# Attention scores in 64-row halves of the TensorE array, the band mask added by VectorE with the maximum, value products in alternating column halves

## The chip, the cores and the metric

The kernel runs on one core of a Trainium2 chip. A core has five engines with queues of their own: TensorE (matrix products, called PE in the profile; its weight loads are PEld), VectorE (DVE), ScalarE (ACT), GpSimd (POOL) and SyncE (SP, which here only starts DMAs). Each engine works through its own queue in the order in which the program was laid out, and waits on semaphores for the others. Products land in PSUM, everything else lies in SBUF. The metric is the time of one execution on the device in microseconds; the lower, the better. Three runs of the kernel before gave 1540.58 us in the median.

## What is computed

Two layers of a hybrid trunk on 128 context tokens (the prompt) and 256 latent tokens (the sample). Each layer is a feed-forward block, a mixing block of attention, convolution and long convolution, and a second feed-forward block. The change touches the attention alone: eight query heads in two groups of four that share one key and one value head, with 64 features each.

```python
# context tokens (block 0): 128 queries x 128 keys, no mask
s = jnp.einsum('bqgrd,bkgd->bgrqk', qblk, k).astype(F32) * scale
p = softmax(concat([s, sink]))[..., :-1]
o = jnp.einsum('bgrqk,bkgd->bqgrd', p, v)
# latent tokens (blocks 1 and 2): 128 queries x (local keys within +-128, and 128 cached keys)
band = jnp.abs(kj[None, :] - BLOCK - qi[:, None]) <= WINDOW
s_loc = jnp.where(valid, s_loc, NEG_INF)        # valid: band and inside the sequence
p = softmax(concat([s_loc, s_ctx, sink]))
o = p[local] @ v + p[context] @ v_cached
```

All inputs are fp32.

## The kernel before

Prompt and sample are handled together: 384 token columns, features on the 128 partitions. All large products are split into a high and a low part of fp32r and need three passes (`mm3`, L252 to L256); their weights come as a stream of 313 chunks of 512 KB, which ScalarE (L240) and VectorE (L241, `lo`) split. The attention products are plain fp32; TensorE takes such a product in two passes, each with its own weight load, so the profile shows two rows for one call.

A Tile scheduler lays out each engine's order from the priorities of the code and its own estimate of durations. Within the mixing block `PROGRAM` (L41) interleaves generators by hand: input projections, the long convolutions (`hyena`, H, and `conformer`, C, with Fourier products at L633 and L679), scores (A), values (V) and the output projection (W).

`attn_k` (L763) makes the keys. `ks` holds the rotated sample keys and the cached keys for blocks 1 and 2, `kp` the prompt keys for block 0. Each has a slot for each key head g, in which the 64 partitions of the other head are zero: GpSimd clears both tiles (L771, L772), then the real halves are filled.

`scores` (L792) runs over three blocks b of 128 queries and four pairs of heads j. The query tile `st["q"][j]` holds head j of group 0 in partitions 0 to 63 and of group 1 in 64 to 127. With the zero-padded keys, a product over all 128 partitions gives the scores of one group.
- Block 0: one product with 256 columns gives both groups (L804); one VectorE maximum (L818).
- Blocks 1 and 2: for each group a product with 384 columns (L809) and one with the identity that adds the 128x128 mask to one third of it (L810). Both go to an `S` buffer in PSUM, of which there are two. VectorE takes the maximum of each (L820).

VectorE then forms the exponent's bias (L821), and ScalarE reads the scores from PSUM, writes the exponential to `P` and sums it up (L825). An `S` buffer comes free when that is read. When the four pairs are done, the sums are inverted, and VectorE and ScalarE multiply the probabilities (L837, L839).

`values` (L842) runs over the blocks b and their key blocks k (1, 3 and 3). For each group g, TensorE transposes four heads' probabilities into an `at` buffer (L858), and ScalarE copies that to `pt` (L861). Then, for each g, one product with 512 columns (L865) writes 64 of the 128 PSUM partitions: the two groups use the left and the right 64 columns of the array (`tile_position=(0, 64 * g)`). After the last k, ScalarE and VectorE split the result for the output projection (L869, L870).

## Time and profile before

| | |
|---|---|
| median of three runs | 1540.58 us (1539.62 to 1542.72) |
| span of the profiled execution | 1540.7 us |
| TensorE busy (products / weight loads) | 1503.2 us / 1427.3 us |
| VectorE, ScalarE, GpSimd busy | 1117.8, 671.4, 29.8 us |
| attention of layer 0 and layer 1 | about 411 to 491 us and 1144 to 1224 us |

The span is counted from the first to the last instruction of the profiled execution. A row of a group names the line of the kernel, the engine, the operation, what is written and what is read, the size, how often it ran, its busy time and the mean duration of one. Rows of the timeline give the start and the duration of an instruction or of some like ones that were merged. TensorE's ends are modelled, and its products are pipelined: the distance of starts tells more than a duration. Busy time counts moments in which two instructions of one engine overlap once.

### The profile page before, as it was taken

The page shows a single profiled execution, that of the slowest core. Times are in us where ns is not written, and L with a number is a line of the kernel's source. Part 1 is how long each engine was busy: PE and PEld are TensorE (multiplying, and loading weights), DVE is VectorE, ACT ScalarE, POOL GpSimd, SP SyncE. Part 2 cuts the span into 40 slices and gives each one's busy share as a digit, 9 for nine tenths or more (in the row PEclk, how much of TensorE's full clock was granted, in tenths as well). Part 3 has the DMA queues.
Part 4 walks back from the last instruction along what each step waited for, and adds up shares of the span by engine and source line. Part 5 has one row for each costly group of instructions (what it writes and reads, how often), then busy time and mean ns, then how long its engine had stood idle before and what let it go on. Part 6 is the DMA issues. An engine that isn't in the chain of part 4 may idle for free.

```text
span 1540.7 us, 22275 instructions
## 1 busy us (share of the span) xinstructions
PE 1503.2 (98%) x8466; PEld 1427.3 (93%) x8466; DVE 1117.8 (73%) x2082; ACT 671.4 (44%) x1160; POOL 29.8 (2%) x75
## 2 busy tenths in 40 slices
PE   6999999999999999999999999999999999999997
PEld 2799999999977999989999998999997799999997
DVE  5799898886984788886657988766599577655332
ACT  5673332335475562333336322333447556333332
POOL 0101000000000000000000000000000000000000
PEclk9999999999999999999999999999999999999998
DMA  7847776665311347676443777654431134454431
GB/s 277 313 134 259 238 239 225 209 212 171 112 58 57 121 151 236 215 231 206 151 151 121 233 225 227 219 178 152 146 120 62 55 110 148 154 164 151 123 123 41
DMA packets 72122, 258.80 MB, mean 168 GB/s; under 512 B 8176, under 2 KB 9712, under 8 KB 72016
## 3 DMA queue, kind: packets, MB, share of 16 engines
q1 hardware_dynamic: 70832, 252.14, 51.2%
q0 software_dynamic: 1184, 5.24, 0.9%
q8 instruction: 66, 1.08, 0.3%
q14 instruction: 40, 0.33, 0.1%
HBM read 250.80 MB, written 6.55 MB: 167 GB/s over the span
## 4 chain that ended last, share of the span: by engine, by line
PE 67%; DMA 14%; DVE 13%; issue 3%; ACT 1%; SPq 0%; DVEq 0%; POOLq 0%; ACTq 0%
DMA raw<-wmod 13%; PE acc L254 12%; PE acc L256 12%; PE acc L255 12%; PE S L254 7%; PE S L256 7%; PE S L255 7%; DVE junk L315 6%; DVE lo L241 4%; PE sp L633 2%; PE S L809 1%; PE sp L679 1%; DVE t L494 1%; PE acc L865 1%; PE sp L926 1%
## 5 line engine op out<-in xcount | busy, mean ns | idle before, releaser
L241 DVE TENSOR_TENSOR lo<-raw,hi 128x1024 fp32r<-128x1024 f32 x313 | 381.9, 1222 | 173.1 <-ACT hi L240 171.1
L240 ACT CAST hi<-raw 128x1024 fp32r<-128x1024 f32 x313 | 327.1, 1047 | 395.2 <-issue 154.2
L315 DVE SCALAR_TENSOR_TENSOR junk<-raw,cb 128x1024 f32<-128x1024 f32 x256 | 312.8, 1222 | 69.9 <-DMA raw<-wmod 67.6
L256 PE MATMUL acc<-h,lo 128*128 128x384 f32 (+1 forms) x960 | 326.6, 340 | 8.3 <-DVE lo L241 8.3
L254 PE MATMUL acc<-h,hi 128*128 128x384 f32 (+1 forms) x960 | 330.6, 345 | 2.2 <-ACT hi L240 2.1
L255 PE MATMUL acc<-h,hi 128*128 128x384 f32 (+1 forms) x960 | 324.8, 339 | 0.0
L256 PE MATMUL S<-h,lo 128*128 128x384 f32 (+1 forms) x768 | 259.6, 338 | 0.1
L254 PE MATMUL S<-h,hi 128*128 128x384 f32 (+1 forms) x768 | 259.6, 338 | 0.0
L255 PE MATMUL S<-h,hi 128*128 128x384 f32 (+1 forms) x768 | 258.9, 337 | 0.0
L256 PEld LDWEIGHTS acc<-h,lo 128*128 128x128 f32 x960 | 181.2, 189 | 14.1 <-DVE lo L241 13.6
L254 PEld LDWEIGHTS acc<-h,hi 128*128 128x128 f32 x960 | 180.5, 188 | 7.2 <-ACT hi L240 3.2
L255 PEld LDWEIGHTS acc<-h,hi 128*128 128x128 f32 x960 | 180.6, 188 | 1.8 <-issue 0.2
L256 PEld LDWEIGHTS S<-h,lo 128*128 128x128 f32 x768 | 144.7, 188 | 1.9 <-DVE lo L241 1.1
L254 PEld LDWEIGHTS S<-h,hi 128*128 128x128 f32 x768 | 144.2, 188 | 0.6 <-issue 0.3
L255 PEld LDWEIGHTS S<-h,hi 128*128 128x128 f32 x768 | 144.3, 188 | 0.0
L384 ACT ACTIVATE h<-x,mod 128x128 fp32r<-128x128 f32 x96 | 41.5, 453 | 83.0 <-DVE x L426 80.2
L494 DVE TENSOR_TENSOR t<-S,t 128x384 f32<-128x384 f32 x72 | 39.9, 554 | 33.6 <-PE S L256 33.6
L272 ACT CAST P<-t 128x384 fp32r<-128x384 f32 x24 | 12.3, 513 | 81.7 <-DVE t L494 81.7
L256 PE MATMUL acc<-P,lo 128*128 128x384 f32 x120 | 40.6, 338 | 0.4 <-DVE lo L241 0.4
L254 PE MATMUL acc<-P,hi 128*128 128x384 f32 x120 | 40.6, 338 | 0.0
L255 PE MATMUL acc<-P,hi 128*128 128x384 f32 x120 | 40.5, 338 | 0.0
L385 DVE SCALAR_TENSOR_TENSOR h<-x,mod,h 128x128 fp32r<-128x128 f32 x96 | 38.4, 415 | 1.2
(348 smaller groups left out, 2268.9 us busy)
## 6 DMA issues: line engine op xcount, KB each, us to landing
raw<-stream SPq DMA_DIRECT2D x313, 512.0 KB, 3.7
raw<-wmod SPq DMA_DIRECT2D x128, 512.0 KB, 4.5
raw<-wms SPq DMA_DIRECT2D x16, 512.0 KB, 6.7
Hd<-sw POOLq DMA_DIRECT2D x6, 768.0 KB, 6.2
H<-Hd SPq DMA_DIRECT2D x6, 768.0 KB, 5.0
x<-x SPq DMA_DIRECT2D x8, 192.0 KB, 6.5
y<-h SPq DMA_DIRECT2D x6, 256.0 KB, 2.6
cb<-crow SPq DMA_DIRECT2D x2, 512.0 KB, 9.0
```

The source lines that it names most:

```text
L240: nc.scalar.copy(out=hi, in_=raw)
L241: nc.vector.tensor_tensor(out=lo, in0=raw, in1=hi.bitcast(F32), op=ALU.subtract)
L254: nc.tensor.matmul(out, lhsT=w[0], rhs=x[0], start=start, stop=False)
L255: nc.tensor.matmul(out, lhsT=w[0], rhs=x[1], start=False, stop=False)
L256: nc.tensor.matmul(out, lhsT=w[1], rhs=x[0], start=False, stop=stop)
L315: nc.vector.scalar_tensor_tensor(out=self.junk, in0=raw, scalar=1.0, in1=self.cb[:, ci, :], op0=ALU.mult, op1=ALU.mult, accum_out=m[:, 2 * ...
L384: nc.scalar.mul(out=hl[:, 0, a:b], in_=self.x[k][:, a:b], mul=sc)
L385: nc.vector.scalar_tensor_tensor(out=hl[:, 1, a:b], in0=self.x[k][:, a:b], scalar=sc, in1=hl[:, 0, a:b].bitcast(F32), op0=ALU.mult, op1=AL ...
L494: nc.vector.tensor_tensor(out=s, in0=up[:, :T], in1=s, op=ALU.mult)
L633: self.nc.tensor.matmul(U[:, ri * 256:ri * 256 + 256], lhsT=self.cst(("fw", t), 128 * ri, 128)[:k], rhs=src[ri], start=True, stop=True)
L679: nc.tensor.matmul(ps[:, t * 128:(t + 1) * 128], lhsT=Y[t][:, k:k + 128], rhs=self.cst(("iv", t), 128 * ri, 128), start=ri == 0, stop=ri == 1)
L809: nc.tensor.matmul(S[g], lhsT=lhs, rhs=kz[:, g, :], start=True, stop=False)
```

## The change

1. `attn_k` keeps one key tile without padding: key head 0 in partitions 0 to 63, key head 1 in 64 to 127. The two clears on GpSimd, two of four rope sums on VectorE, two of four copies and two of four cache loads in both layers fall away.
2. `scores` takes, for each group g, only the partitions 64g to 64g + 63 of queries and keys, in the upper or the lower 64 rows of the array (`tile_position=(64 * g, 0)`). Block 0 has two products with 128 columns in two `S` buffers in place of one with 256.
3. The mask products with the identity go. VectorE adds the mask with the maximum in one instruction (`tensor_tensor_reduce`, shown as ISA, with a second row for the accumulator) and writes the masked scores to `P`. The exponential then reads `P` in SBUF and no longer PSUM, so the `S` buffer comes free with VectorE's read. The constants hold one row of masks with 640 columns, out of which each block takes 384.
4. `values` splits each product into two of 256 columns, in the order half h = 0 of g = 0 and 1, then half h = 1 of g = 0 and 1.
5. The second product of a pair (and the second to fourth of a value group) has a priority that is raised by 400, and the first one waits by an added dependence (`after`) for the last read of the pair before (scores) or for the second `pt` copy (values). Both together place the members of a group next to each other in TensorE's order.

```diff
+PAIR = 400
-    put("mask0", np.where(q[None, :] <= q[:, None], 0.0, -1e30))
-    put("mask1", np.where(q[None, :] >= q[:, None], 0.0, -1e30))
+    z = np.zeros((128, 128))
+    put("mask", np.concatenate([np.where(q[None, :] >= q[:, None], 0.0, -1e30), z, z,
+                                np.where(q[None, :] <= q[:, None], 0.0, -1e30), z], axis=1))
...
+    def after(self, inst, other):
+        if other is not None:
+            self.tc.add_manual_dep(inst.ins, other.ins.name,
+                                   mybir.DependencyInfo(mybir.DependencyClass.Sync, mybir.DependencyReason.DATA),
+                                   reason="pairs of row or column tiles issue together")
...
-        ks = self.S("kv", (128, 2, NS + PAST))
+        ks = self.S("kv", (128, NS + PAST))
         st["kv"] = self.S("kv", (128, 768))
...
+        kp = st["kv"][:, 0:NP]
+        nc.scalar.copy(out=kp, in_=kr[:, 0:NP])
+        nc.gpsimd.dma_start(out=ks[:, NS:NS + PAST], in_=self.d["ck"][l])
+        self.rope(kr[:, NP:T], [(slice(0, 128), ks[:, 0:NS])])
...
-                if b == 0:
-                    t = self.psum("S")[:, :256].rearrange("p (g k) -> p g k", g=2)
-                    nc.tensor.matmul(t, lhsT=lhs, rhs=kz, start=True, stop=True)
-                    S = [t[:, 0, :], t[:, 1, :]]
-                else:
-                    S = [self.psum("S")[:, :nk * 128] for _ in range(2)]
-                    for g in range(2):
-                        nc.tensor.matmul(S[g], lhsT=lhs, rhs=kz[:, g, :], start=True, stop=False)
-                        nc.tensor.matmul(S[g][:, 128 * (2 - b):128 * (3 - b)], lhsT=self.ident,
-                                         rhs=self.cst("mask%d" % (b - 1)), start=False, stop=True)
+                S = [self.psum("S")[:, :nk * 128] for _ in range(2)]
+                for g in range(2):
+                    p = slice(64 * g, 64 * g + 64)
+                    with self.tc.high_priority(offset=PAIR * g):
+                        mm = nc.tensor.matmul(S[g], lhsT=st["q"][j][p, b * 128:(b + 1) * 128], rhs=kz[p], start=True,
+                                              stop=True, tile_position=(64 * g, 0))
+                    if g == 0:
+                        self.after(mm, read)
...
-                if b == 0:
-                    nc.vector.tensor_reduce(out=mx, in_=t, axis=AX.X, op=ALU.max)
-                for g in range(2) if b else ():
-                    nc.vector.tensor_reduce(out=mx[:, g:g + 1], in_=S[g], axis=AX.X, op=ALU.max)
+                for g in range(2):
+                    if b:
+                        read = nc.vector.tensor_tensor_reduce(out=P[:, g, :], in0=S[g],
+                                                              in1=self.cst("mask", 256 * (2 - b), 384), scale=1.0,
+                                                              scalar=-3.0e38, op0=ALU.add, op1=ALU.max,
+                                                              accum_out=mx[:, g:g + 1])
+                        S[g] = P[:, g, :]
+                    else:
+                        nc.vector.tensor_reduce(out=mx[:, g:g + 1], in_=S[g], axis=AX.X, op=ALU.max)
...
-                    nc.scalar.copy(out=pt, in_=tp)
+                    copied = nc.scalar.copy(out=pt, in_=tp)
                     pts.append(pt)
                 vi = 0 if b == 0 else 1 + k
-                for g in range(2):
-                    nc.tensor.matmul(o[64 * g:64 * g + 64, :], lhsT=st["vt"][:, vi, 64 * g:64 * g + 64], rhs=pts[g],
-                                     start=k == 0, stop=k == nk - 1, tile_position=(0, 64 * g))
+                for h in range(2):
+                    c = slice(256 * h, 256 * h + 256)
+                    for g in range(2):
+                        with self.tc.high_priority(offset=PAIR * (h + g > 0)):
+                            mm = nc.tensor.matmul(o[64 * g:64 * g + 64, c], lhsT=st["vt"][:, vi, 64 * g:64 * g + 64],
+                                                  rhs=pts[g][:, c], start=k == 0 and h == 0, stop=k == nk - 1,
+                                                  tile_position=(0, 64 * g), skip_group_check=True)
+                        if h + g == 0:
+                            self.after(mm, copied)
```

Outside the two mixing blocks the order of TensorE is the same. Within them it moves. Three places follow; one row there is one call (two passes on TensorE for the fp32 products), the line numbers are those of the kernel in question, and a number after a tile's name tells its buffers apart. TensorE, layer 0, around the values of block 0 (`acc_4164`) and the second score pair of block 1 (`S_4091`, `S_4092`), before:

```order
L858 MATMUL at_4172<-csts,P_4025 128x128
L353 MATMUL sp_4270<-ones,cv_4072 128x1 x3
L865 MATMUL acc_4164<-pt_4170,kv_3740 64x512
L865 MATMUL acc_4164<-pt_4177,kv_3740 64x512
L254 MATMUL acc_4226<-h_2510,hi_4229 128x386
L809 MATMUL S_4091<-kv_3739,q_3687 128x384
L810 MATMUL S_4091<-csts 128x128
L809 MATMUL S_4092<-kv_3739,q_3687 128x384
L810 MATMUL S_4092<-csts 128x128
L255 MATMUL acc_4226<-h_2510,hi_4229 128x386
```

The same place after, where the values are `acc_4165`, that score pair is `S_4096` and `S_4097`, and `S_4151` and `S_4152` are the next pair:

```order
L867 MATMUL at_4173<-csts,P_4031 128x128
L810 MATMUL S_4096<-kv_3739,q_3687 128x384
L810 MATMUL S_4097<-kv_3739,q_3687 128x384
L877 MATMUL acc_4165<-pt_4171,kv_3740 64x256
L877 MATMUL acc_4165<-pt_4178,kv_3740 64x256
L877 MATMUL acc_4165<-pt_4171,kv_3740 64x256
L877 MATMUL acc_4165<-pt_4178,kv_3740 64x256
L361 MATMUL sp_4269<-ones,cv_4079 128x1 x3
L810 MATMUL S_4151<-kv_3739,q_3919 128x384
L810 MATMUL S_4152<-kv_3739,q_3919 128x384
```

The score pair has moved ahead of the value products, without the mask products (L810 of before), and the four value pieces stand in alternating halves. VectorE, layer 0, the maxima of that second pair, before:

```order
L820 TENSOR_REDUCE st_4084<-S_4091 128x1
L668 TENSOR_TENSOR ut_4010<-ut_4010 128x256
L820 TENSOR_REDUCE st_4084<-S_4092 128x1
L669 TENSOR_TENSOR ut_4010<-sw_4042 128x256
L821 SCALAR_TENSOR_TENSOR st_4084<-st_4084,nsink_77 128x2
```

And after:

```order
L821 ISA P_4100,st_4089<-S_4096,csts 128x384
L821 ISA st_4089 128x1
L673 TENSOR_TENSOR sw_4049<-sp_4059,H_4015 128x512
L675 TENSOR_TENSOR ut_4014<-sp_4059,H_4015 128x512
L821 ISA P_4100,st_4089<-S_4097,csts 128x384
L821 ISA st_4089 128x1
```

Two 512-column products of the long convolution now stand between the pair's two reads. TensorE, layer 0, the second key block of the values of block 1 (`acc_4282` from `pt_4367` and `pt_4374`), before:

```order
L865 MATMUL acc_4282<-pt_4367,kv_3740 64x512
L809 MATMUL S_4404<-kv_3739,q_3921 128x384
L810 MATMUL S_4404<-csts 128x128
L254 MATMUL sp_4378<-cv_4352,hi_4382 128x384
L254 MATMUL sp_4379<-cv_4352,hi_4382 128x384
L809 MATMUL S_4405<-kv_3739,q_3921 128x384
L865 MATMUL acc_4282<-pt_4374,kv_3740 64x512
```

And after, where they are `acc_4281` from `pt_4366` and `pt_4373`:

```order
L867 MATMUL at_4415<-csts,P_4196 128x128
L877 MATMUL acc_4281<-pt_4366,kv_3740 64x256
L877 MATMUL acc_4281<-pt_4373,kv_3740 64x256
L877 MATMUL acc_4281<-pt_4366,kv_3740 64x256
L877 MATMUL acc_4281<-pt_4373,kv_3740 64x256
L867 MATMUL at_4422<-csts,P_4090 128x128
```

The two halves, which stood five products apart, now stand together. Such a separation is found three times in the order before (once in layer 0, twice in layer 1) and not in the order after.

## Rows read from the trace of the kernel before

**Rows 1.** The page's first part: busy us, share of the span, instructions

```profile
PE 1503.2 (98%) x8466; PEld 1427.3 (93%) x8466; DVE 1117.8 (73%) x2082; ACT 671.4 (44%) x1160; POOL 29.8 (2%) x75
```

**Rows 2.** Busy us by stretch: PE, PEld, DVE, ACT, POOL, then PE clock, DMA

```profile
431.00:451.00 20.00, 20.00 (x102) 15.86 (x101) 17.92 (x44) 14.65 (x46) 0.89 (x1) 1.00 0.01 5
451.00:471.00 20.00, 19.35 (x101) 13.12 (x99) 16.00 (x45) 15.15 (x40) 0.00 (x0) 1.00 0.18 54
471.00:491.00 20.00, 19.09 (x94) 12.82 (x94) 7.71 (x20) 11.09 (x27) 0.00 (x0) 1.00 0.17 52
1164.00:1184.00 20.00, 19.58 (x97) 15.10 (x96) 18.37 (x45) 15.07 (x45) 1.24 (x1) 1.00 0.09 27
1184.00:1204.00 20.00, 20.00 (x105) 13.29 (x104) 15.71 (x47) 15.52 (x41) 0.56 (x1) 1.00 0.09 27
```

**Rows 3.** TensorE's waits, 395 to 530 us: total us, times, longest

```profile
PE acc L254 <- DVE h L870: 0.9, 1, 0.9
```

**Rows 4.** TensorE's timeline: one score pair of block 1, one of block 0

```profile
442.13 0.81 PE L809 MATMUL S<-kv,q 128*128 128x384 f32 x2
...
443.00 0.81 PE L809 MATMUL S<-kv,q 128*128 128x384 f32 x2
443.65 0.38 PE L810 MATMUL S<-csts 128*128 128x128 f32 x2
...
1144.61 0.59 PE L804 MATMUL S<-kv,q 128*128 128x256 f32 x2
1145.04 0.38 PE L633 MATMUL sp<-ut,csts 128*128 128x256 f32 x1
```

**Rows 5.** TensorE's timeline: products in four column quarters, at the start

```profile
25.24 0.64 PE L284 MATMUL at<-raw,scond 128*32 128x256 f32 x8
25.81 0.70 PE L926 MATMUL sp<-kv,cv 128*128 128x512 f32 x1
```

**Rows 6.** TensorE's timeline: products that use 8 of the rows

```profile
62.60 0.34 PE L256 MATMUL acc<-h,lo 128*128 128x386 f32 x1
62.77 0.34 PE L256 MATMUL S<-h,lo 128*128 128x386 f32 x1
63.04 0.69 PE L633 MATMUL sp<-P,csts 8*128 8x256 f32 x2
...
64.44 0.59 PE L633 MATMUL sp<-cv,csts 8*128 8x256 f32 x2
64.96 0.44 PE L254 MATMUL acc<-h,hi 128*128 128x386 f32 x1
```

**Rows 7.** Timeline: a joint value group, then one half that stands alone

```profile
1217.44 1.07 ACT L861 COPY pt<-at 128x512 f32<-128x512 f32 x2 [1.80 <-PE at L858]
...
1218.08 1.56 PE L865 MATMUL sp<-pt,kv 128*64 128x512 f32 x4
1218.57 0.19 PEld L865 LDWEIGHTS sp<-pt,kv 128*64 128x64 f32 x2 [0.30 <-ACT pt L861]
1219.57 0.31 PEld L858 LDWEIGHTS at<-csts,P 128*128 128x128 f32 x3 [0.81 <-issue]
...
1195.26 1.07 PE L865 MATMUL acc<-pt,kv 128*64 128x512 f32 x2
1196.26 0.33 PE L858 MATMUL at<-csts,P 128*128 128x128 f32 x1
```

**Rows 8.** VectorE: two groups by line and form, then its timeline

```profile
L820 DVE TENSOR_REDUCE st<-S 128x1 f32<-128x384 f32 x32 | 17.6, 554 | 7.5 <-PE S L810 6.8
L315 DVE DVE_READ_ACCUMULATOR junk<-raw,cb 128x1 f32 x256 | 21.1, 83 | 0.0
...
455.63 1.73 DVE L837 TENSOR_SCALAR P<-P,st 128x384 f32<-128x384 f32 x5
457.28 0.55 DVE L820 TENSOR_REDUCE st<-S 128x1 f32<-128x384 f32 x1
```

16 lines of the change are left out of this document (5 added, 11 removed).

## Prediction

> **What bounds the kernel now.** I read the page first, then the busy time by stretch around the two attention stages, then what TensorE waited for there, and last single instructions. The page says that TensorE is busy for 98% of the span and VectorE for 73% [rows 1]. Busy alone proves little, so the next view matters more: where the attention of layer 0 (431 to 491 us) and of layer 1 (1164 to 1204 us) lies, TensorE is busy for 19.1 to 20 of every 20 us at a granted clock of 1.00, which is the 2.4 GHz level [rows 2]. The waits agree: in layer 0's stage the longest wait of a TensorE product was 0.9 us, once [rows 3]. So TensorE's queue sets the end, and a microsecond of TensorE work that goes away here brings the end forward by as much, as long as no other engine becomes late. The candidate for that is in the same rows: VectorE is busy for 17.92 of 20 us, then 16.00, then only 7.71; in layer 1 18.37 in the first such stretch [rows 2]. The order of TensorE outside the two stages is unchanged, so everything else is taken as it was.
>
> **Scores of blocks 1 and 2 (16 pairs in both layers).** Each fp32 product is two passes. Before, one head pair is two times (a 384-column product over a zero-padded K and a 128-column mask product with the identity). The row starts 442.13 and 443.00 give 0.87 us for one group of heads, 1.73 us for both, and of that the two 384-column passes take 0.65 us (443.00 to 443.65), 0.32 us each [rows 4]. The change drops the mask products and puts the two groups into the upper and lower 64 rows of the array. What remains is two 384-column products in different halves. If the halves run side by side this is 2 x 0.32 = 0.65 us, and no longer 1.73.
>
> Side by side is not shown for row halves, but it is for column quarters and halves: eight 256-column passes in four column quarters took 0.57 us to the next instruction, where one after the other eight of 0.21 us would be 1.7 us [rows 5]. And in the value product the second column half's weight load started at 1218.57, 0.05 us after the end of the copy that it reads (1217.44 plus two copies in 1.07 us would be 1218.51), while the first half was still in its second pass [rows 7]. So a half waits for its data and not for the other half.
>
> Against this stands a price that the old scores didn't pay: a change of the array's partition. It can be read where the kernel multiplies only 8 rows, which also uses a part of the rows. Full-array passes follow each other at 0.17 us (62.60 to 62.77), so the last one ends near 62.94; the next row starts at 63.04, and it lasts 0.10 us longer than the same pair later, which is its weight load. That is 0.20 us of nothing. On the way back the last part-row pass, of which two together take 0.43 us, ends near 64.87, and the next full one streams from 64.96 + 0.10, as it too lasts 0.10 us longer than its like at 62.77: 0.20 us [rows 6]. Together 0.40 us for each visit. In between, passes of 256 columns came 0.215 us apart, so weight loads stay hidden in that mode.
>
> A pair therefore costs 0.65 + 0.40 = 1.05 us instead of 1.73: 0.68 us saved, 16 times, 10.9 us of TensorE work. "TensorEngine Tiling (Array Packing)" of the Trainium skill (Tiling Modes, Key Properties) says the same against this change: switching the tiling mode drains TensorE. The trace agrees and prices it, 0.40 us for a visit.
>
> **Scores of block 0 (8 pairs).** Before, one 256-column product: 0.43 us from 1144.61 to 1145.04 [rows 4]. After, two of 128 columns side by side, 0.22 us, plus 0.40: 0.62. This part loses 0.2 us each, 1.6 us in all: the zero padding was cheaper than the switch.
>
> **Values (14 groups: one and three and three key blocks in two layers).** They already sit in column halves, so the switch is paid now too. A joint group takes 1.49 us from 1218.08 to 1219.57; a half that stood alone took 1.00 us from 1195.26 to 1196.26 [rows 7]. In the new order the four 256-column pieces always stand together and the first waits for the second copy, so both halves start together and need what one half needs, 1.0 us. That is 0.49 us for each of the 11 groups that stood together. In the order, 3 groups had their halves apart (one is shown); each pays two visits of about 1.2 us, and 1.2 us goes. Sum 11 x 0.49 + 3 x 1.2 = 9.0 us. The cover it needs: while the second copy (0.5 us) is under way, TensorE must have something else; at the places that I read in the order a score pair (1.05 us) or four transposes stand there. Without that cover the 0.49 us is not saved, since today's group also ends 1.0 us after the second copy. The split into column halves itself should give nothing, as the halves overlap already.
>
> **VectorE.** 32 maxima of 384 columns (0.55 us each) become 32 add-and-max instructions of the same size with an accumulator read. The nearest row for an operation that also accumulates is the modulation product with its read of 83 ns [rows 8]. Instructions overlap: five that began at 455.63 end 1.73 us later, at 457.36, and the next starts at 457.28, so one occupies about 0.08 us less than its duration [rows 8]. I take 0.47 us as before plus 0.08 us: 0.55. The lower bound is 0.47 (the read is hidden), the upper one twice the columns' time, 0.95 us (a sum and a maximum in two passes, as two separate rows would take). Added to VectorE: 32 x 0.08 = 2.6 us; the eight block-0 maxima become 16 of half the size, which adds about 1 us; four rope sums become two of full height, which takes off half as much. ScalarE's exponentials read the masked copy: no change taken, as ScalarE is at 73 to 78% of these stretches [rows 2]. GpSimd loses four clears, SyncE's constant load grows by 384 columns far ahead of its use: nothing.
>
> **What TensorE's savings run into.** The new order makes the first half of a pair wait until both maxima of the pair before are read, and TensorE's queue is in order: the weights' products, transposes and value products behind it wait too. By the order of VectorE, one or two 512-column spectral products stand between the two reads. So I take the stage in stretches.
>
> The block-0 stretch loses 4 x 0.2 = 0.8 us in each layer. In 431 to 471 us there are 7 pairs (4.8 us) and two joint and one split group (2.2 us): TensorE's work falls from 40 to 33.0 us. VectorE has 17.92 + 16.00 = 33.9 us there [rows 2], with 14 x 0.08 more 35.0. So VectorE becomes the limit, and the stretch can't be shorter than 35.0. It has been 90% busy in a stretch in which TensorE waited for nothing, and I take 95% for one in which TensorE does wait: 35.0 / 0.95 = 36.9, a gain of 3.1 of the 7.0 us. The bounds are 0 and 5.0. From 471 to 491 VectorE is at 39%, and one pair and four groups give their full 0.68 + 4 x 0.49 = 2.6 us. Layer 0: -0.8 + 3.1 + 2.6 = 4.9 us. Layer 1 has VectorE at 18.37 and 15.71 [rows 2], 34.1 us, and the same pieces in slightly other places (two split groups, one group fewer behind): 3.1 again, 2.2 behind, 4.5 us. Sum 9.4 us.
>
> The profiled execution has a span of 1540.7 us and the median is 1540.6, so the sum needs no correction: **1531 us**.
>
> **Rivals.**
> - *A half starts only after the other's last pass has started.* Then a pair is three passes, 0.97 + 0.40 = 1.37 us, and block 0 pays 0.1 us more each. "TensorE: Matmul & The Clock Gate" (Part 3) states such an order: matmuls start and end strictly in program order. The row of 1218.57 doesn't decide it, as that half waited for its copy. In the long stretch TensorE would need 7 x 0.32 = 2.3 us more, 35.3, about what VectorE needs, so some 0.5 us more a layer; with 0.3 us behind and 0.4 us of block 0 that is 2.4 us in both layers: 1533.5.
> - *Row halves don't overlap.* Four passes and a switch, 1.69 us, save 0.04 us a pair, and block 0 costs 0.83 instead of 0.43. Long stretch 0.3 + 2.2 = 2.5, behind 2.0, block 0 -1.6: 2.9 us a layer, 1535. The column rows [rows 5] speak against it.
> - *The waits for the pair's reads eat the whole of the long stretch.* Left are -0.8 + 2.4 us a layer: 1537.4. For it speaks that VectorE is already at 80 to 92% there; against it that the score bank is now free after the maximum and no longer after the exponential, which comes later.
> - *Slower: the add-and-max is a long instruction.* Every pair waits for two of them, so VectorE's 33.9 us grow by 14 times the extra. At 0.95 us instead of 0.47 that is 40.6 us, at 95% 42.8: 2.8 us lost, with block 0 and the end of the stage +1.2 us a layer, 1543. At 1.35 us it is 46.2, or 48.7: +7 us a layer, 1555. It decides from about 0.85 us an instruction. Nothing in the trace has such a length for 384 columns (0.55 us is usual), but this instruction is not in the trace.
>
> **How the numbers follow.** A measurement of this kernel tells 0.2% (3.1 us) from no change. Forecast (1526 to 1534): 0.46; the ordered start 0.10; no overlap 0.10; waits eat it 0.17; slower 0.14; VectorE packs without a gap (5.0 instead of 3.1 us and shorter waits for copies, 1525 or below) 0.03. Of the eaten case, 0.04 lies below 1537.5 and 0.13 around no change; of the slower one 0.01 lies within 0.2%. Faster 0.46 + 0.10 + 0.10 + 0.03 + 0.04 = 0.73, same 0.14, slower 0.13. The range 1525 to 1541 leaves out 0.03 below and 0.13 above.
>
> **What the profile after would show.** Right: the two halves' starts of a pair some 10 ns apart, the pair over 1.1 us after the last full pass; value groups 1.0 us each; VectorE at 95% in the long stretch and TensorE's waits there naming the new add-and-max line, 3 to 5 us a layer; the rest of the kernel shifted without change. Wrong: starts of the second half 0.32 us (ordered) or 0.65 us (no overlap) later; the add-and-max near 1 us; or waits of 7 us and more in a layer.

## The result and the profile after

The changed kernel takes 1519.5 us (median of 4 executions, 1515.2 to 1519.9) beside 1540.1 us for the kernel before on the same chip: a ratio of 0.985, 95% interval 0.984 to 0.987. That is 20.6 us less where the forecast had 9.6 less; the range 1525 to 1541 missed it on the fast side. The profiled execution took 1519.2 us with a span of 1517.4 us, 23.3 us under the span before.

The first page line after answers [rows 1]: TensorE is busy for 16.8 us less, VectorE as long as before.

```profile
PE 1486.4 (98%) x8474; PEld 1416.0 (93%) x8474; DVE 1116.1 (74%) x2120; ACT 671.6 (44%) x1158; POOL 26.8 (2%) x69
```

The busy time by stretch answers [rows 2] (columns as there: PE, PEld, DVE, ACT, POOL, then PE clock, DMA share, GB/s). The stages come earlier now, layer 1's by about 20 us.

```profile
431.00:451.00 20.00, 19.08 (x101) 12.38 (x99) 19.99 (x67) 16.84 (x48) 1.93 (x1) 1.00 0.09 27
451.00:471.00 20.00, 19.09 (x119) 14.49 (x118) 17.81 (x57) 17.98 (x49) 0.00 (x0) 1.00 0.09 27
471.00:491.00 20.00, 19.84 (x127) 17.10 (x125) 8.67 (x20) 10.14 (x20) 0.00 (x0) 1.00 0.32 99
1144.00:1164.00 20.00, 18.80 (x92) 12.63 (x92) 17.84 (x52) 13.90 (x41) 0.00 (x0) 0.91 0.08 27
1164.00:1184.00 20.00, 17.40 (x103) 10.62 (x102) 16.21 (x55) 16.97 (x46) 0.89 (x1) 1.00 0.09 27
1184.00:1204.00 20.00, 19.57 (x121) 15.73 (x120) 9.74 (x26) 11.51 (x27) 0.00 (x0) 1.00 0.25 80
```

VectorE fills 37.8 of the 40 us from 431 to 471 us (95%), and TensorE, which was busy for 39.4 of them before, now stands idle for 1.8. In layer 1 the idle share is larger, and the granted clock of 1144 to 1164 us is 0.91 where it was 1.00 throughout.

Single instructions on TensorE (start, duration, operation) answer [rows 4] and [rows 7]: a score pair of block 1, a pair of block 0, and a value group.

```profile
433.21 0.34 PE L262 MATMUL acc<-h,hi 128*128 128x386 f32 x1
433.39 0.34 PE L263 MATMUL acc<-h,hi 128*128 128x386 f32 x1
433.67 0.92 PE L810 MATMUL S<-kv,q 64*128 64x384 f32 x4
434.51 0.44 PE L264 MATMUL acc<-h,lo 128*128 128x386 f32 x1
434.79 0.34 PE L262 MATMUL acc<-h,hi 128*128 128x386 f32 x1
...
408.37 0.34 PE L264 MATMUL acc<-h,lo 128*128 128x386 f32 x1
408.64 0.49 PE L810 MATMUL S<-kv,q 64*128 64x128 f32 x4
409.06 1.13 PE L641 MATMUL sp<-ut,csts 128*128 128x256 f32 x4
...
473.04 1.08 PE L877 MATMUL sp<-pt,kv 128*64 128x256 f32 x8
474.05 0.66 PE L867 MATMUL at<-csts,P 128*128 128x128 f32 x4
```

Full passes follow each other at 0.18 us (433.21 to 433.39), so the next was due at 433.57. The pair starts 0.10 us later, takes 0.84 us, and the pass behind it lasts 0.10 us longer than its like (434.51 to 434.79): 1.04 us from one regular pass to the next. In the unmerged records the two halves' first passes start 6 to 7 ns apart, then both second ones 0.43 us later. A block-0 pair takes 0.42 us and 0.10 on entry. A value group takes 1.01 us.

VectorE (first the instructions of the add-and-max line with least, median and longest ns, then its timeline) answers [rows 8]:

```profile
L821 DVE CUSTOM_DVE_ANT_0 P<-S,csts x32: 544/550/558, 435.5 to 1186.1; 128x384 f32<-128x384 f32 x32
L821 DVE DVE_READ_ACCUMULATOR2_ANT st<- x32: 77/83/85, 435.9 to 1186.6; 128x1 f32 x32
...
445.30 0.56 DVE L821 CUSTOM_DVE_ANT_0 P<-S,csts 128x384 f32<-128x384 f32 x1
445.78 0.08 DVE L821 DVE_READ_ACCUMULATOR2_ANT st<- 128x1 f32 x1
445.78 0.55 DVE L821 CUSTOM_DVE_ANT_0 P<-S,csts 128x384 f32<-128x384 f32 x1
```

The add-and-max is as long as the old maximum (550 against 554 ns), and the read of its accumulator runs beside the next instruction: 0.48 us from start to start.

**Where the time went.** I compare when the same weight product starts in both traces (7512 of them, in the same order). The difference, after minus before, at the edges of the stretches:

| stretch (us of before) | what runs there | shift at its end, us | gained there, us |
|---|---|---|---|
| 0 to 396 | start, first feed-forward | -3.1 | 3.1 |
| 396 to 503 | mixing with attention, layer 0 | -11.0 | 7.9 |
| 503 to 906 | feed-forward (the gain lies in 636 to 720) | -13.5 | 2.6 |
| 906 to 991 | feed-forward, layer 1 | -20.8 | 7.3 |
| 991 to 1097 | feed-forward | -20.8 | 0.0 |
| 1097 to 1235 | mixing with attention, layer 1 | -23.3 | 2.5 |
| 1235 to the end | feed-forward | -23.3 | 0.0 |

The two mixing blocks give 10.4 us. The other 12.9 us come from stretches in which not one instruction was changed or moved, but for the longer load of the constants in the first. The 3.1 us of the first stretch say nothing, though: in a second profiled execution of the changed kernel (a_same, below) that stretch was 3.0 us longer than before. The granted clock stood at the 1.2 GHz level (0.50) for 10.2 us of it, against 3.4 us in the execution above. What is left to explain are 9.9 us in 636 to 720 and 906 to 991 us. The waits (who waited for whom, total us, times, longest) of 906 to 991 us show what went there. The kernel before:

```profile
PEld acc L256 <- DVE lo L241: 6.5, 8, 1.0
...
DVE junk L315 <- DMA raw<-wmod: 11.5, 9, 2.0
```

The kernel after, in the same work at 892 to 970 us; TensorE has no wait there:

```profile
DVE junk L323 <- DMA raw<-wmod: 5.8, 9, 1.0
```

VectorE's modulation products wait for the modulation weights' transfer, behind them in VectorE's queue stand the low parts of the streamed weights, and TensorE waits for these. With the transfers a little earlier the chain no longer reaches TensorE. In 636 to 720 us the same wait of TensorE falls from 5.4 to 3.0 us. So there were two questions: why transfers land earlier, and what the three edits are worth by themselves.

### The profile page after: what moved, and what is told of

Same layout as the page of the kernel before. It is cut to its first block, busy times and chain, and to the rows that moved or that the text cites. A ratio compares the mean times of both kernels' runs of the same rounds, so it can differ in the third digit from the quotient of the medians.

```text
span 1517.4 us, 22303 instructions
## 1 busy us (share of the span) xinstructions
PE 1486.4 (98%) x8474; PEld 1416.0 (93%) x8474; DVE 1116.1 (74%) x2120; ACT 671.6 (44%) x1158; POOL 26.8 (2%) x69
## 4 chain that ended last, share of the span: by engine, by line
PE 74%; DVE 10%; DMA 9%; issue 3%; ACT 2%; SPq 0%; DVEq 0%; POOLq 0%; ACTq 0%
PE acc L262 13%; PE acc L264 13%; PE acc L263 13%; PE S L262 9%; PE S L264 9%; PE S L263 9%; DMA raw<-wmod 9%; DVE junk L323 4%; DVE lo L249 3%; PE sp L641 2%; PE sp L941 1%; PE sp L687 1%; PE S L810 1%; DVE t L502 1%; PE acc L877 0%
## 5 line engine op out<-in xcount | busy, mean ns | idle before, releaser
L262 PEld LDWEIGHTS S<-h,hi 128*128 128x128 f32 x768 | 144.2, 188 | 0.6 <-issue 0.5
L264 PE MATMUL acc<-P,lo 128*128 128x384 f32 x120 | 40.6, 338 | 0.4 <-DVE lo L249 0.4
L262 PE MATMUL acc<-P,hi 128*128 128x384 f32 x120 | 40.6, 338 | 0.0
L263 PE MATMUL acc<-P,hi 128*128 128x384 f32 x120 | 40.5, 338 | 0.0
```

Of the source, the lines that this page charges most:

```text
L262: nc.tensor.matmul(out, lhsT=w[0], rhs=x[0], start=start, stop=False)
L263: nc.tensor.matmul(out, lhsT=w[0], rhs=x[1], start=False, stop=False)
L264: nc.tensor.matmul(out, lhsT=w[1], rhs=x[0], start=False, stop=stop)
```

## Experiments: the gain outside the attention

The only thing in the change that reaches these stretches is the size of the constants: 384 columns more, which lengthens one load, moves every SBUF tile behind them by 1536 bytes, and makes one HBM array 192 KB larger. Four kernels take this apart.

**b_wide.** The kernel before, with dead columns:

```diff
     put("mask1", np.where(q[None, :] >= q[:, None], 0.0, -1e30))
+    put("pad", np.zeros((128, 384)))
     main = off
```

> The kernel before with nothing of the change but the size of its constants: 384 dead columns behind the masks, so that the constants are 2821 columns wide in SBUF and 3205 in HBM, as in the changed kernel, and every tile behind them lies at the changed kernel's address. No instruction differs but the late load of the constants, 1920 columns instead of 1536. Theory A (the 12.8 us outside the two attention stages come from where the data lie): 1540.1 - 12.8 = about 1527, and the stretch from 906 to 991 us loses its waits of TensorE for weights. Theory B (they come from the changed instructions, by way of what runs beside them or before them): 1540, within 2.

Measured: 1527.4 us, ratio 0.993 (0.990 to 0.995). Theory A, and B is out: with none of the edits 11 us are gone.

**b_hbm** and **b_sbuf** split the two places. In b_hbm the same `put` stands behind `zT`, which is never loaded into the constants' tile; in b_sbuf:

```diff
+        self.pad = cp.tile([128, 384], F32, name="pad")
+        nc.gpsimd.memset(self.pad, 0.0)
         nc.sync.dma_start(out=self.csts[:, 0:128], in_=self.d["cst"][:, 0:128])
```

> The kernel before with 384 dead columns at the end of the constants' HBM array alone, never loaded: HBM sizes as in the changed kernel, SBUF as in the kernel before. Theory A1 (place in HBM): about 1527. Theory A2 (place in SBUF) and theory B (instructions): 1540, within 2.

> The kernel before with an unused SBUF tile of 384 columns between the constants and the tiles behind them: SBUF addresses as in the changed kernel, HBM as in the kernel before (one fill by GpSimd at the start is added). Theory A2 (place in SBUF): about 1527. Theory A1 (HBM) and theory B (instructions): 1540, within 2.

Measured: b_hbm 1531.3 us, ratio 0.996 (0.994 to 0.998); b_sbuf 1539.5 us, ratio 1.000 (0.999 to 1.002). It is HBM, not SBUF. b_hbm ranges from 1527 to 1541, more than the others.

**a_narrow** is the change without the larger array: the two triangles stay in the constants as before, and GpSimd puts the mask together once, in a tile behind all others:

```diff
+            self.mask = self.mp.tile([128, 640], F32, name="mask")
+            nc.gpsimd.memset(self.mask, 0.0)
+            nc.gpsimd.tensor_copy(out=self.mask[:, 0:128], in_=self.cst("mask1"))
+            nc.gpsimd.tensor_copy(out=self.mask[:, 384:512], in_=self.cst("mask0"))
```

> The changed kernel with the constants of the kernel before, in size and place: the 640-column mask is put together by GpSimd, once, in a tile behind all others (one of the ten 2-column buffers goes to make room). All instructions of the other engines as in the changed kernel. Theory A (place of the data): the gain outside the stages goes, 1519.5 + 12.8 = about 1532, which is 1540.1 less the stages' 10.4 with the start's share. Theory B (instructions): 1519.5, within 2.

Measured: 1529.3 us, ratio 0.994 (0.992 to 0.996), 9.2 us under the kernel before on its chip (1538.5). The mixing blocks give 7.8 and 2.6 us as in the changed kernel. So the edits are worth 9 us and the larger array the rest.

**More of the same.** If the size of one array does that, other sizes and other arrays should tell more. a_hbm2 is the changed kernel with `put("pad", np.zeros((128, 384)))` behind `zT`; b_hbm128 is the kernel before with 128 such columns.

> The changed kernel with 384 more dead columns at the end of the constants' HBM array, never loaded; every instruction and every SBUF address as in the changed kernel. Theory P (the place of the arrays in HBM sets how many packets are slow, by size in no order that can be foreseen): the time moves by several us from 1519.5, up to 1530, together with the 99th percentile of the 4 KB packets (787 ns after the change, 927 before). Theory Q (the larger array is better by its size or row pitch as such): 1519.5 or less. If neither place nor size counted: 1519.5, within 2.

> The kernel before with 128 dead columns at the end of the constants' HBM array, a third of what the change adds (64 KB); nothing else differs. Theory P (place in HBM, every shift its own draw): anything from 1527 to 1540, and the 99th percentile of the 4 KB packets goes with it (740 ns at 1531, 927 at 1540). If the effect needs the whole 192 KB: 1538 to 1540.

Measured: a_hbm2 1528.1 us, ratio 0.992 (0.990 to 0.995), so it takes 8.6 us longer than the change with every instruction the same; b_hbm128 1530.3 us, ratio 0.994 (0.992 to 0.996). A larger array isn't better as such, and the first 64 KB bring what 192 KB bring.

Four more ask whether it is the place of the arrays. b_own and b_x put 192 KB elsewhere, b_rows into more rows instead of wider ones, and b_order declares the weight stream before all other arrays.

The pieces of b_own (whose load takes the first 256 columns), b_rows and b_x, in this order:

```diff
-    hw12 = np.zeros((128, 256), np.float32)
+    hw12 = np.zeros((128, 640), np.float32)
...
-        "cst": CST_ARR,
+        "cst": np.concatenate([CST_ARR, np.zeros((18, CST_ARR.shape[1]), np.float32)]),
...
-        "x": np.ascontiguousarray(xs.T.reshape(KT, 128, T)),
+        "x": np.concatenate([xs.T.reshape(KT, 128, T), np.zeros((1, 128, T), np.float32)]),
```

> The kernel before, constants untouched; the 384 dead columns (192 KB, never loaded) stand in another HBM array instead, the filters' first weights, which is loaded once at the start. Theory P (place: whatever makes the arrays behind it lie elsewhere changes the share of slow packets): a time other than 1540, likely 1527 to 1533, with the 99th percentile of the 4 KB packets well under 900 ns. Theory Q (it is the constants' own array, its row pitch): 1540, within 2, and 900 ns or more.

> The kernel before, all arrays at their own sizes, but the weight stream's array (160 MB) declared first in HBM instead of last. No instruction differs. Theory P: the time may move by several us either way, with the slow packets. Theory Q (sizes, not places): 1540, within 2. If arrays are not placed in the order of declaration, 1540 says nothing.

> The kernel before with 18 dead rows (203 KB) behind the constants' 128 rows in HBM: the array grows as in the changed kernel, but its row pitch stays 11,284 bytes. Theory pitch (the wider rows count): 1540, within 2, with a 99th percentile of the 4 KB packets of about 900 ns. Theory size (the array's size counts, by what it does to the arrays around it): a time of 1527 to 1532, with 740 to 790 ns.

> The kernel before with one dead tile (192 KB) at the end of the input array that is declared right behind the constants. Theory place (all arrays behind the constants move by 192 KB): 1527 to 1532, and 740 to 790 ns. Theory Q (the constants' array alone counts, whatever lies behind it): 1540, within 2, and about 900 ns, as with the same 192 KB in the filters' weights.

Measured: b_own 1541.1 us (ratio 1.001, 0.999 to 1.002) and b_order 1538.8 us (1.000, 0.999 to 1.001) change nothing; b_rows 1530.8 us (0.994, 0.992 to 0.996) and b_x 1529.9 us (0.993, 0.992 to 0.994) do what the change did. So it isn't the rows' pitch, and not the constants' array alone: the same 192 KB in the input array (1.6 MB) work, in a weight array of 128 KB they don't. The waits of b_x in the stretch of above (its 900 to 981 us; the same instructions as before):

```profile
PEld acc L256 <- DVE lo L241: 1.0, 1, 1.0
...
DVE junk L315 <- DMA raw<-wmod: 7.1, 7, 1.6
```

TensorE's wait falls from 6.5 to 1.0 us, and the stretch from 85.8 to 79.7 us. Where the time stayed, so did the wait: 5.5 us in b_own, 4.8 in a_narrow, 5.9 in a_hbm2. What the transfers did can be counted from the trace's packet records: each profiled execution moves 58,752 packets of 4 KB on the main queue, and their median is 159 ns everywhere. What differs is the tail.

| kernel | HBM | median us | 99th percentile, ns | packets over 0.8 us |
|---|---|---|---|---|
| before | constants as before | 1540.1 | 927 | 1054 |
| b_sbuf | as before | 1539.5 | 898 | 918 |
| b_own | +192 KB in a 128 KB array | 1541.1 | 884 | 902 |
| b_order | stream declared first | 1538.8 | 907 | 952 |
| a_narrow | as before | 1529.3 | 901 | 925 |
| b_hbm128 | +64 KB | 1530.3 | 740 | 419 |
| b_hbm | +192 KB | 1531.3 | 740 | 412 |
| b_wide | +192 KB | 1527.4 | 785 | 541 |
| b_rows | +203 KB as rows | 1530.8 | 782 | 534 |
| b_x | +192 KB in the input | 1529.9 | 767 | 479 |
| after | +192 KB | 1519.5 | 787 | 530 |
| a_hbm2 | +384 KB | 1528.1 | 1001 | 1398 |

Packets over 0.8 us number 900 to 1050 with the old sizes, 410 to 540 with 64 to 203 KB more (376 to 561 with the kernels of the next section) and 1400 with the last, whatever the kernel. The two stretches with modulation loads go with them: set against the kernel before, they are together 0.8 to 3.8 us shorter with the old sizes, 8.3 to 12.1 us with 64 to 203 KB more and 1.1 us with the last. That a size in HBM sets both is shown, since in b_hbm, b_hbm128, b_rows and b_x nothing else differs. That the tail is what sets the stretches is argued: both move together, but not in proportion, for a_hbm2 has a third more of these packets than the kernel before and is no slower there. Why a size does this is open: where the arrays come to lie can't be read from a trace, and b_own and b_order say that declared order and a shift of the later arrays alone don't describe it.

**a_same** is the changed kernel once more, on the chip of the later experiments.

> The changed kernel once more, beside the others on their chip: how far one program's time moves with the chip and the call. If the draw of slow packets belongs to the program: 1519.5 within 2, ratio 0.985. If it belongs to the chip or the call: up to 1530. Measured beside it, the kernel without the row halves was at 1516.1, ratio 0.985.

Measured: 1522.5 us (1518.0 to 1525.6), ratio 0.989 (0.987 to 0.991), with 507 packets over 0.8 us. The tail belongs to the program. Some 3 us of the time do not: the executions of this run had a mean granted clock of 0.991 to 0.996, those of the first 0.994 to 0.997. a_hbm2 lies 5.6 us above this time, taken on its own chip, and 8.6 above the first.

## Experiments: what the edits are worth

All of these have the changed kernel's array sizes, so b_wide (1527.4 us) is their base. Beside the times, the table gives what TensorE spent from start to start of its products in the two mixing blocks together, by what the product is. A wait counts to the product that ran before it. The last column is the part of the first that the granted clock took: half of the time for which it stood at the 1.2 GHz level (0.50) in the two blocks. Each row is one profiled execution; after and a_same are the same program and differ by 1.5 us, about what the clock took more (1.7). b_wide and the kernel before agree in every cell to 0.1 us.

| kernel | both blocks, us | weight products | scores and mask | transposes | value products | rest | taken by the clock |
|---|---|---|---|---|---|---|---|
| before | 245.5 | 142.0 | 30.3 | 13.1 | 22.6 | 37.5 | 0 |
| after | 235.1 | 142.0 | 18.2 | 18.8 | 15.5 | 40.5 | 1.7 |
| a_same | 236.6 | 143.1 | 18.4 | 18.8 | 15.5 | 40.8 | 3.4 |
| s_wide | 237.6 | 140.7 | 17.4 | 16.8 | 20.8 | 41.9 | 0 |
| v_wide | 241.6 | 144.2 | 30.8 | 14.0 | 14.6 | 38.0 | 0 |
| m_wide | 234.7 | 140.0 | 22.6 | 13.6 | 21.1 | 37.3 | 0 |
| h_wide | 251.9 | 141.0 | 26.2 | 18.5 | 22.1 | 44.3 | 5.1 |
| mv_wide | 231.3 | 143.1 | 21.6 | 14.5 | 14.6 | 37.4 | 0 |
| a_nodep | 244.9 | 143.8 | 24.3 | 15.1 | 22.3 | 39.5 | 6.8 |
| a_norm | 234.6 | 141.2 | 17.4 | 20.4 | 15.1 | 40.6 | 0 |

**s_wide** and **v_wide**, the two halves of the change: the changed kernel with `values` as before, and b_wide with `values` as after.

> The score part alone: constants, keys, row halves and the add-and-max of the changed kernel, values in joint 512-column products as in the kernel before; constants of the changed size, so b_wide (1527.4) is the base and the change's whole gain over it is 7.9. Theory T (each part keeps what TensorE saves): 16 pairs x (1.73 - 0.85) = 14.1 us, so 1513. Theory V (VectorE and ScalarE set the pace of the stages once the scores are short, so the two parts' gains overlap): 5 to 8 us, 1519.5 to 1522.5, which leaves little for the values. Theory S (the parts share the gain as the forecast did, 9.3 to 9.0): about 4, 1523.5.

> The value part alone: 256-column value products in alternating column halves, scores and mask as in the kernel before; constants of the changed size, base b_wide (1527.4). Theory T: the whole 9.0 us of TensorE, 1518.5. Theory V: 3 to 6 us, 1521.5 to 1524.5, and with the score part's gain more than the 7.9 to 10.4 of both together. Theory S: about 4, 1523.5. A rival to all: without the shorter scores the second copy of probabilities is late for the group as before, and the gain is under 2.

Measured: s_wide 1520.6 us, ratio 0.988 (0.986 to 0.990), 7.9 us off the blocks; v_wide 1526.6 us, ratio 0.992 (0.990 to 0.994), 3.9 us off the blocks, of which 0.8 show in the median. By the blocks that is theory V for both: the value products take 7.9 us less, and half of it comes back as waits of TensorE elsewhere. By its median v_wide is where the rival is, but for another reason than the rival's, since its value groups did shrink to 14.6 us.

**m_wide**, the mask alone, and **h_wide**, the row halves alone:

First m_wide against b_wide (its add-and-max is the changed kernel's), then h_wide against s_wide:

```diff
-                        nc.tensor.matmul(S[g], lhsT=lhs, rhs=kz[:, g, :], start=True, stop=False)
-                        nc.tensor.matmul(S[g][:, 128 * (2 - b):128 * (3 - b)], lhsT=self.ident,
-                                         rhs=self.cst("mask%d" % (b - 1)), start=False, stop=True)
+                        nc.tensor.matmul(S[g], lhsT=lhs, rhs=kz[:, g, :], start=True, stop=True)
```

```diff
+                for g in range(2) if b else ():
+                    nc.tensor.matmul(S[g][:, 128 * (2 - b):128 * (3 - b)], lhsT=self.ident,
+                                     rhs=self.cst("mask", 384 * (2 - b)), start=False, stop=True)
...
+                        read = nc.vector.tensor_reduce(out=mx[:, g:g + 1], in_=S[g], axis=AX.X, op=ALU.max)
...
-                    if b == 0:
-                        read = e
+                    read = e
```

In the last lines `e` is the exponential: a pair of h_wide waits for the exponentials of the pair before.

> The mask alone moved to VectorE: the two identity products of a pair go, the add-and-max comes, the scores stay full-array products with zero-padded keys; no tile modes change. Constants of the changed size, base b_wide (1527.4). TensorE's pair 1.73 - 2 x 0.22 = 1.29, so 16 x 0.44 = 7.0 us less. Theory T: 1520.4. Theory V: 3 to 5 us, 1522.5 to 1524.5. If the add-and-max costs VectorE more than the maximum did (against the 0.476 us from start to start seen after the change), the time is at or above 1527.4.

> The row halves alone: scores in 64-row halves as in the changed kernel, but the mask still added on TensorE by two full-array identity products, and VectorE's plain maximum; values in joint products. Constants of the changed size, base b_wide (1527.4). The kernel with the mask alone moved took 5.4 and 5.5 us off the two stages, as much as the whole change. Theory M (the mask's move is what counts, the halves' saving turns into waits of TensorE for probabilities, and each pair now also switches modes twice): 0 to 2 us, 1525.5 to 1527.5. Theory T (the halves save (30.3 - 6.4 - 18.2) = 5.7 us of TensorE in both layers and keep it): about 1522.

Measured: m_wide 1516.3 us (1513.1 to 1523.9), ratio 0.986 (0.983 to 0.988); h_wide 1535.5 us, ratio 0.997 (0.996 to 0.999). The mask alone takes 10.8 us off the blocks, all that the whole change takes and more than theory T had: 7.7 us in the column of scores and mask, the rest mostly behind weight products (2.0) and value products (1.5). The row halves alone add 6.4 us to the blocks and 8.1 us to the median (a ratio of 0.997 beside 0.993). Both theories for the halves were too kind. Their waits name one reason (h_wide, TensorE, layer 0's block, then layer 1's):

```profile
PE S L810 <- ACT P L831: 2.7, 2, 2.5
...
PE S L810 <- ACT P L831: 3.5, 2, 2.0
```

A pair needs both score banks free, and with the mask on TensorE a bank is free only after ScalarE's exponential has read it. With the masked copy in SBUF it is free after VectorE. The granted clock is the other reason. It fell in both blocks where TensorE idled (h_wide, columns as in the stretches above), and took 5.1 of the 6.4 us:

```profile
455.00:460.00 5.00, 2.53 (x11) 1.58 (x11) 5.00 (x16) 4.02 (x12) 0.00 (x0) 0.85 0.34 102
...
1180.00:1185.00 5.00, 3.52 (x16) 2.39 (x16) 4.47 (x15) 4.37 (x11) 0.00 (x0) 0.71 0.00 0
```

So the earlier bank pays where row halves want both at once. That it pays without them isn't shown: in the kernel before, whose products take one bank each, TensorE idled ahead of those of L809 for the exponential's end for 0.4 us in all. What m_wide gained beyond the mask's own products was not taken apart.

**mv_wide** leaves the row halves out: the mask on VectorE, the values as after, scores as full products over padded keys.

> The mask moved to VectorE and the values in alternating column halves, scores as full-array products with padded keys: the change without its row halves. Constants of the changed size. Theory M (TensorE is no longer what the stages wait for once the mask's products are gone): within 2 of the kernel with the mask alone, 1514.5 to 1518.5, no slower than the change's 1519.5. Theory T (TensorE's time still counts): the value groups took 15.5 instead of 22.6 us after the change, so up to 7 less, about 1510. If the halves of the scores are needed as cover for the second copy of probabilities, the value groups stay above 20 us and the time at 1516.

Measured: 1516.1 us (1515.9 to 1516.3), ratio 0.985 (0.983 to 0.987); the blocks take 231.3 us, 14.2 less than before and 3.8 less than the whole change. Mask and values add up (10.8 + 3.9 = 14.7); the row halves take 3.8 us of it away again, 1.7 of them by the granted clock. s_wide and m_wide, neither of which has such a fall there, differ by 2.9 us for the same step. In the block of layer 1 the clock fell in six of the eight profiled executions with row halves (not in s_wide and a_norm) and in none of the twelve without. Beside the changed kernel's 1519.5 and 1522.5 us mv_wide is, with m_wide's 1516.3, the lowest of all, though the ratios' intervals overlap with the first of these. By its time that is theory M: the values' 3.4 us less in the blocks than m_wide don't show in the median. A score product in it, on TensorE:

```profile
441.73 0.34 PE L264 MATMUL acc<-h,hi 128*128 128x386 f32 x1
441.91 0.81 PE L818 MATMUL S<-kv,q 128*128 128x384 f32 x2
442.26 0.63 PE L265 MATMUL acc<-h,lo 128*128 128x386 f32 x1
442.73 0.34 PE L263 MATMUL acc<-h,hi 128*128 128x386 f32 x1
```

From 441.91 to 442.73 is 0.82 us with one weight pass (0.18) in it: 0.64 us a product, 1.29 a pair, and no 0.10 us on the way in. Each product also stands where its own bank is free, one by one between weight passes. The row halves' pair, 1.04 us, is only 0.25 us shorter and must find both banks free. Ahead of score pairs, beyond the usual distance, TensorE lost 4.6 us in both blocks after the change (24 pairs, about half of it the 0.10 on entry); ahead of score products it lost 0.9 in mv_wide.

**a_nodep** drops the two added dependences (`self.after(...)`), **a_norm** gives ScalarE four of the ten reciprocal products of VectorE in each layer (`DVE_NORM = [[], [4, 2, 7], [5, 1, 4]]`).

> The changed kernel without the two added dependences that hold back a pair's first row half until the buffers of both are free, and a group's first column product until both copies are done; the halves keep their priorities. Theory D (waiting for both buffers is what eats the row halves' gain: 2.3 us a layer ahead of the pairs after the change, 0.1 of each pair's being the mode switch): the waits ahead fall to about 1.1 a layer and the time to 1517. Theory M (the probabilities set the pace, and pairs that break up lose what they save): 1519 to 1523.

> The changed kernel with four of the ten 128x384 multiplications by the softmax's reciprocal moved from VectorE to ScalarE, in each layer (three and three of eight stay on VectorE instead of five and five). Theory V (after the change VectorE's queue is what TensorE waits for in the stages): 4 x about 0.4 us of VectorE freed a layer, some 1 to 3 us off 1519.5, 1517 to 1518.5. Theory N (it is ScalarE's copies and multiplications that TensorE waits for): 4 x about 0.5 us more on ScalarE a layer, 1520 to 1523. Theory T (neither): 1519.5.

Measured: a_nodep 1523.9 us, ratio 0.990 (0.988 to 0.992); a_norm 1519.5 us, ratio 0.987 (0.985 to 0.989). Without the dependences the waits ahead of scores fall only to 3.6 us, but halves no longer meet: scores 24.3 instead of 18.2 us, values 22.3 instead of 15.5. The blocks lose 9.8 us in the profiled execution, 5.1 of them by the granted clock; that execution took 1530.4 us, 6.5 above the median. The median itself is 1.4 us above a_same's on the same chip, with overlapping ratios. So theory D is out and theory M nearer (1519 to 1523), but that the dependences shorten the kernel is not shown. Moving the multiplications does nothing measurable, so VectorE's load alone isn't what binds after the change, although it is 95% busy.

## Why the prediction was right and wrong

- **The step that failed** is in its first paragraph: "The order of TensorE outside the two stages is unchanged, so everything else is taken as it was", and with it the constants' load "nothing". The order was unchanged, as said; the transfers were not. The kernel before loses up to 6.5 us in one stretch to a chain that starts at a transfer, and 192 KB more in the constants' array, with none of the edits, took 11.1 us off (b_wide). The trace of before had that wait in it, but the prediction read waits only where the edits were. At the old array sizes the size of the forecast holds: a_narrow took 9.2 us off where 9.6 were forecast. That is in part luck, as the layers below show.
- **TensorE sets the end of the stages**: right in direction, not one for one. Removing the mask's products, 6.4 us of TensorE, took 10.8 us off the blocks, so some 4 us were no work of TensorE; 7.9 us less for the value products gave 3.9. [rows 3] has the waits of products alone, not those of weight loads.
- **The base**: 1540.7 us is a span, and a time holds more (1519.2 us for a span of 1517.4 after the change), so the agreement with the median says nothing. The forecast stands on the median and isn't moved by it.
- **Score pairs**: 1.05 us forecast, 1.04 measured. "TensorEngine Tiling (Array Packing)" of the Trainium skill (Tiling Modes) says that a change of mode drains TensorE. The trace agrees. It shows 0.10 us ahead of a pair and 0.10 on the pass behind it, half of the 0.40 forecast for a visit. The other half lies inside: a row-half pass pair takes 0.42 us, where a full-array pass takes 0.32. So the switch was put too high and the pair's passes too low by the same 0.20 us, and the sum is right by luck.
- **Block 0**: 0.62 forecast; 0.42 and 0.10 on entry are seen, 0.52, and what the way out costs there can't be read.
- **Values**: 1.0 us a group forecast, 1.01 measured in twelve of fourteen. The sum is 7.0 us instead of 9.0 in the changed kernel, where one group ran while the clock was low and took 1.90 us, and 7.9 in v_wide, mv_wide and a_narrow. The three split groups gave 1.0 us each and not 1.2: their halves had taken 1.00 us each. That the split into column pieces by itself gives nothing wasn't tried.
- **VectorE**: 0.55 us for the add-and-max, 0.48 measured; the accumulator's read is hidden, which was the lower bound. The slower rival, from 0.85 us, is out.
- **What the savings run into**: 18.3 us of TensorE saved and 9.4 kept was the sum; the table has 19.1 us (12.1 on scores and mask, 7.0 on values) and 10.4, or 8.9 in a_same. The 19.1 is not quite the forecast's term: the 0.10 us on either side of a visit, up to 4.8 us for 24 pairs, counts in the table to the products around a pair. Of what didn't last, 1.7 us are the clock's. The size kept was near and the cause half right. The waits that name the add-and-max line are 4.2 us in both layers (2.8 of weight loads, 1.4 of products, partly the same time), not 3 to 5 in each. By the table, time grew behind transposes (5.7 us) and in the rest (3.0), and a_norm says that relieving VectorE doesn't return it. Which link of that chain of VectorE and ScalarE ends last was not settled.
- **The layers**: 4.9 and 4.5 us forecast, 7.9 and 2.5 measured, 7.9 and 1.0 in a_same. Why layer 0 gained more was not tried; the shorter add-and-max fits. In layer 1 TensorE idled for 1.14 of 5 us, and the granted clock fell behind it, partly to the 1.2 GHz level (same columns as the stretches above):

```profile
1150.00:1155.00 5.00, 3.86 (x22) 2.28 (x24) 4.83 (x15) 3.91 (x12) 0.00 (x0) 0.92 0.02 3
1155.00:1160.00 5.00, 5.00 (x24) 3.12 (x21) 3.65 (x14) 3.52 (x11) 0.00 (x0) 0.74 0.00 0
```

  That is 8% and 26% of 5 us, 1.7 us of TensorE's time, and a score pair in it took 1.44 us to the next product where others take 0.85. a_narrow shows the same fall (0.95 and 0.71 in 1160 to 1170 us), and a_same one of 3.4 us. Without it layer 1 gave 4.2 and 4.4 us, close to the forecast, which had taken the clock at 1.00 throughout. The sum came out because layer 0 gave 3 us more and the clock took some 2 us back. mv_wide, whose TensorE had 19.89 us of work in the like stretch, kept a clock of 1.00 there.
- **The ordered start** is out: the second half's first pass starts 7 ns after the first half's, 0.42 us ahead of that half's second pass. "TensorE: Matmul & The Clock Gate" (Part 3) of the Trainium skill has matmuls start and end in program order. By it a pair would have taken three passes, 0.97 us and the switch. The trace doesn't agree for two fp32 products in different halves, if a product's two passes stand next to each other in the program, which the trace doesn't tell. "No overlap" is out by the same rows.

## What to carry to other kernels

Before an edit is credited with a gain, compare when the same untouched instruction starts in both traces: here about half of it came from stretches that were not edited, and dead columns in an HBM array alone gave or took 6 to 11 us. Compare the granted clock of the two traces as well, before waits are blamed: in h_wide it took 5.1 of 6.4 us. Where transfers stand just behind a queue that TensorE waits for, an array's size belongs to the change and should be held fixed in an experiment. And of three edits made together one (the mask added where the maximum is read) carried the stages' gain, a second (the value pieces) added to it in the blocks but hardly in the medians, and the third (the row halves) took some away, which only taking them apart shows.

## What was not expected of the hardware

- The size of one HBM array changes the slow tail of all 4 KB packets (902 to 1054, 376 to 561 or 1398 over 0.8 us, of 58,752) and leaves their median at 159 ns; the same bytes in a 128 KB array change nothing (902).
- Two row halves run side by side, but not at full pace: 0.42 us for a pass of 384 columns in each, 0.32 for one in the full array. Two full-array products cost 1.29 us, two row halves 1.04 with the switch.
- An addition with a maximum and an accumulator over 128x384 costs VectorE what the maximum alone does (550 ns against 554), and the read of the accumulator runs beside the next instruction.
- The granted clock fell to the 1.2 GHz level in the layer-1 block of six of the eight profiled executions with row halves and of none of the twelve without. In the changed kernel it fell at 1154.2 us, behind 4.2 us in which TensorE idled for 1.14.
